# Compact chunk operands and alternating heads in the mixing stage of a flow step, with new orders in the front, the turns and the end

## The chip, the cores and the metric

The kernel runs on one core of one Trainium2 chip. The metric is the device time of one execution in microseconds (us). TensorE (PE, with its weight loads PEld) does the matmuls and the transposes, VectorE is DVE, ScalarE is ACT, GpSimd is POOL, and SyncE (SP) issues nearly all transfers.

## The reference

The reference is one inference step of a hybrid backbone for 512 latent tokens and 128 context tokens, T = 640 in all, with D = 2048. Cut to what matters:

```python
def _layer(x, mod, s0, shift_fn, lp):
    sh1, sc1, g1, sh2, sc2, g2 = jnp.split(mod, 6, axis=-1)
    h = _rmsnorm(x, lp['norm1_g']) * (1.0 + sc1) + sh1
    p = h @ lp['w_in']
    o_a, s_fin = _rwkv7_bidir(shift_fn(p[..., :C_SHIFT], lp['mu_shift']), s0, lp)
    o_b = _chunk_gmlp(jax.nn.gelu(p[..., C_SHIFT:]), lp)
    x = x + g1 * (jnp.concatenate([o_a, o_b], axis=-1) @ lp['w_out'])
    h = _rmsnorm(x, lp['norm2_g']) * (1.0 + sc2) + sh2
    ff = (jax.nn.silu(h @ lp['w_ffn_gate']) * (h @ lp['w_ffn_up'])) @ lp['w_ffn_down']
    return x + g2 * ff, s_fin
# mod = silu(c) @ w_mod + b_mod; y = _rmsnorm(x, final_norm_g)
# _rwkv7_bidir: 16 heads of 64, per direction S = S*w + (S a) b^T + v k^T, y = S r
```

## The kernel before, in words

Features lie on the 128 partitions and tokens along the free axis, in two halves of 320 (`HALF`). Most products of weights are made in three: `split` cuts a weight tile into a high and a low part, the activations have `h_hi` and `h_lo`, and `win` adds hi·hi, hi·lo and lo·hi in one PSUM tile (L188 to L190, tile `big`).

**Front.** Five token blocks are loaded and normalised (`xall`, the loop over `t`); each gets its factor `rs` from a power on GpSimd (`rsqrt`, L135), and is transposed to `xnT`. Then `quarter(g, j)` makes a quarter of the shift (g=0) or scale (g=1) of the modulation, from four `w_mod` tiles of 1 MB (L304, pool `wmp`, five buffers). `products(j)` multiplies the first blocks of `w_in`. TensorE's order is written by hand in this stage. `rows()` issues twenty small loads of parameter rows on SP at j = 1, and `params()` transposes them at j = 2.

**Mixing.** While the remaining blocks of `w_in` run as `big` products, three `Mixer` queues hand out the work on the blocks already there in small pieces between them: `take_k` makes the operands of one pair of heads and both directions, `solve` and `merge` (`pblk`, `pM`, `pT`) work on the chunks' triangular systems. A scheduler then fixes the order of the instructions on each engine. A pair of heads lies on 64 + 64 partitions; the ten chunks have 64 tokens. `R` holds two 64-wide operands of a chunk, and `XZ` (L507) the two others for each head, with zeros on the other head's partitions, so that `pG` (L636) multiplies over all 128 partitions. `pXT` (L653) are transposes of one head's rows of `XZ`, `pW` (L664) products of 64 x 64. `pmm` and `pwa` are the products for the norms and for the low-rank weights. All five take one-bank PSUM tiles of pool `pk`, which has two; a piece with both heads takes one for each. ScalarE and VectorE copy the results out (`GB`, `GR`, `GA`, `XT`, `Z`).

**FFN.** Gate, up and down are computed with seven products instead of eight for each 2 x 2 block (`seven`, products 1 to 7 in order `PORD`). The down product runs over six groups `c` of hidden blocks and eight output pairs `n`, 48 steps in all. In the last step of a group (the turn, s % 8 == 7) the operands `xd` of the next group are made: `load` brings them, `put_in` splits them, `turn_ops` says at which product. `Last` combines the seven products of the last group, `later` holds its second half (`out`, `rows`) until a product of the next step.

**End.** Sums of squares of all tokens (`sse`) are added, `rsqrt` makes `rse`, and ten outputs of 128 x 1024 follow: six on VectorE (L1976), four on ScalarE and GpSimd (L1973, L1974).

Of the kernel before, what the change touches and what calls it, by code (L numbers as in the profile page):

```python
# [57 lines left out]
FRONT = 4  # L58
REST = 6
# [28 lines left out]
def flow_step(ctx: ExitStack, tc, x_prompt, x_sample, state_rwkv, c, c_ctx, w_mod, b_mod,  # L88
# [115 lines left out]
    with ExitStack() as ph:  # L204
# [29 lines left out]
        xnT = p0.tile([P, KB, T], F32, name="xnT")  # L234
        for t in range(NT):
            xt = xall[:, t, :]
            ss = p0b.tile([P, 1], F32, name="ss")
            S.activation(junk, xt, AF.Square, accum_out=ss)
            V.tensor_scalar(ss, ss, 1.0 / D, RMS_EPS, op0=ALU.mult, op1=ALU.add)
            rs = p0b.tile([P, 1], F32, name="rs")  # L240
            rsqrt(rs, ss)
            V.tensor_scalar_mul(xt, xt, rs[:, 0:1])
            for q in range(4):
                pt = ps0.tile([P, 4, P], F32, tag="pt", name="ptx")
                for b in range(4):
                    TE.transpose(pt[:, b, :], xt[:, (4 * q + b) * P:(4 * q + b + 1) * P], ident)
                (S.copy if q % 2 else V.tensor_copy)(xnT[:, 4 * q:4 * q + 4, t * P:(t + 1) * P], pt)

# [7 lines left out]

        rowA = p0.tile([P, P], F32, name="rowA")
        rowB = p0.tile([P, P], F32, name="rowB")
        G.memset(rowB, 0.0)
        G.memset(rowA, 0.0)  # L260
        nA = C_W0

        def rows():
            for m in range(4):
                nc.sync.dma_start(rowA[C_MU + 24 * m:C_MU + 24 * m + 24, :],
                                  mu_shift[0, m, 0:3072].rearrange("(r p) -> r p", p=P))
                nc.sync.dma_start(rowA[C_MU2 + 2 * m:C_MU2 + 2 * m + 2, :],
                                  mu_shift[0, m, 3072:3328].rearrange("(r p) -> r p", p=P))
                nc.sync.dma_start(rowA[C_MU3 + m:C_MU3 + m + 1, 0:32], mu_shift[0, m:m + 1, 3328:3360])
            for off, src in ((C_W0, w0[0].rearrange("d (r p) -> (d r) p", p=P)),  # L270
                             (C_A0, a0[0].rearrange("d (r p) -> (d r) p", p=P)),
                             (C_KK, k_k[0].rearrange("(r p) -> r p", p=P)),
                             (C_KA, k_a[0].rearrange("(r p) -> r p", p=P)),
                             (C_RK, r_k[0].rearrange("(r h) n -> r (h n)", h=2)),
                             (C_GW, gn_w[0].rearrange("(r h) n -> r (h n)", h=2)),
                             (C_GB, gn_b[0].rearrange("(r h) n -> r (h n)", h=2)),
                             (C_N2, norm2_g[0].rearrange("(r p) -> r p", p=P))):
                nc.sync.dma_start(rowB[off - nA:off - nA + src.shape[0], :], src)

        def params():  # L280
            pp = ptE.tile([P, 4, P], F32, tag="ptE", name="pp")
            TE.transpose(pp[:, 0, :], rowA, ident)
            TE.transpose(pp[:, 1, :], rowB, ident)
            V.tensor_copy(prm[:, 0:nA], pp[:, 0, 0:nA])
            V.tensor_copy(prm[:, nA:C_N1], pp[:, 1, 0:C_N1 - nA])
            V.tensor_copy(prm[:, C_N2:NPRM], pp[:, 1, C_N2 - nA:NPRM - nA])

        psx.close()
        h_hi = hpool.tile([P, KB, T], F32R, tag="h_hi", name="h_hi")
        h_lo = hpool.tile([P, KB, T], F32R, tag="h_lo", name="h_lo")  # L290
        pe = pex.enter_context(tc.tile_pool(name="pe", bufs=6, space=PSUM))
        early = [[pe.tile([P, HALF], F32, tag="big", name="big") for _ in range(2)] for _ in FIRST]
# [30 lines left out]

        def products(j):
# [8 lines left out]
        for j in range(4):  # L333
            for i, _ in enumerate(itertools.chain(quarter(1, j), quarter(0, j))):
                if i in (2, 3, 4, 6, 7, 8):
                    next(prods, None)
# [10 lines left out]
            if j == 1:  # L347
                rows()
            if j == 2:
                params()  # L350
# [183 lines left out]
    def take_k(pr, p):  # L534
# [19 lines left out]
        pmm([(bones, sq)], lambda ps, s: V.tensor_scalar_max(ssq[:, s], ps, 1e-24), pk)  # L554
# [10 lines left out]
        for d in range(2):  # L565
# [5 lines left out]
            for hf in range(2):  # L571
                s = slice(HALF * hf, HALF * hf + HALF)
                two = [pk.tile([P, HALF], F32, tag="g", name="pwa") for _ in range(2)]
# [45 lines left out]
            V.tensor_mul(rev(XZ[0:64, :, 0, 1, :]), v3(tha)[0:64], i3[0:64])  # L619
# [968 lines left out]
    def seven(b11, b12, b21, b22, x, hook, nk=4, bank=fresh, last=True):  # L1588
# [10 lines left out]
        for o, i in enumerate(PORD):  # L1599
# [12 lines left out]
            if i == 3:  # L1612
                combine(b22, b22, b12)
                combine(b21, b21, b22)
# [393 lines left out]
```

## Time and profile before

| | us |
|---|---|
| median of 3 runs (3287.82 to 3290.53) | 3289.65 |
| profiled execution | 3287.43 |
| its span | 3285.6 |
| mixing stage, 165 to 1060 | 895 |

The rest of the page reads: a busy share for each engine; 40 slices of the span with the granted clock and the GB/s; then groups of instructions by line. In a group, `L636 PE MATMUL pG<-R,XZ` is line, engine, operation, output tile and operands; "x640 | 93.5, 290" is the count, busy us and mean ns of one, and behind the second bar stands the idle time of the engine ahead of them with what ended it. One matmul of full-precision operands has two records. Records of TensorE overlap, so the distance of two starts says more than a duration.

### The profile page before, as it was taken

The numbers are of one execution on the slowest core, as the hardware profiler recorded it, in microseconds if no ns is written. First come the engines' busy times: TensorE is split into PE (matmuls) and PEld (weight loads), VectorE is DVE, ScalarE is ACT, GpSimd is POOL, SyncE is SP. The second block draws the span as 40 slices with busy tenths as digits, with TensorE's granted clock in tenths as the row PEclk, the third lists the DMA queues.
The fourth block names the chain that finished last, engine by engine and source line by source line (L and its number), as shares of the span: only waits on it lengthen the run. The fifth ranks groups of instructions, "written<-read, shape, count | busy, mean of one in ns | idle before, by whom it ended". The sixth has DMA issues, their size and how long they took to land.

```text
span 3285.6 us, 72386 instructions
## 1 busy us (share of the span) xinstructions
PE 3141.3 (96%) x28216; PEld 2905.3 (88%) x28216; DVE 2401.2 (73%) x4152; ACT 1458.3 (44%) x3179; POOL 1260.1 (38%) x1098
## 2 busy tenths in 40 slices
PE   6899999999999999999999999999999999999996
PEld 3688888778887887889899999999999999999996
DVE  4447766776866677767877787777787777877787
ACT  3334444444444444346644444444444444444365
POOL 0001122221222113332166566566565555555543
PEclk9899999999999999999999999999999999999998
DMA  8767776767668588756434433433433454553453
GB/s 318 244 185 219 188 204 188 181 184 206 178 185 222 137 272 277 240 152 182 127 114 120 123 116 116 127 116 116 127 116 116 127 183 149 158 164 122 132 160 119
DMA packets 740142, 550.88 MB, mean 168 GB/s; under 512 B 140712, under 2 KB 673208, under 8 KB 730968
## 3 DMA queue, kind: packets, MB, share of 16 engines
q1 hardware_dynamic: 727480, 532.57, 54.3%
q0 software_dynamic: 9984, 13.13, 1.7%
q8 instruction: 222, 3.64, 0.5%
q14 instruction: 120, 0.98, 0.1%
q10 hardware_dynamic: 2336, 0.57, 0.1%
HBM read 437.79 MB, written 110.95 MB: 167 GB/s over the span
## 4 chain that ended last, share of the span: by engine, by line
PE 75%; DVE 9%; issue 6%; DMA 5%; POOL 3%; ACT 2%; SPq 0%; DVEq 0%; ACTq 0%; POOLq 0%
PE P L1611 15%; PE P L1609 15%; PE P L1610 15%; PE big L188 4%; PE big L190 4%; PE big L189 4%; PE pG L636 2%; PE pm L881 2%; DMA raw<-in_w_in_dram 2%; PE big L1455 1%; PE big L1456 1%; PE big L1457 1%; DMA wt<-in_w_mod_dram 1%; PE pblk L820 1%; DVE mx L781 1%
## 5 line engine op out<-in xcount | busy, mean ns | idle before, releaser
L1611 PE MATMUL P<-xo,lo 128*128 128x320 f32 x2352 | 728.1, 310 | 2.5 <-DVE lo L1397 2.5
L1609 PE MATMUL P<-xo,hi 128*128 128x320 f32 x2352 | 727.4, 309 | 0.7 <-ACT hi L1396 0.7
L1610 PE MATMUL P<-xo,hi 128*128 128x320 f32 x2352 | 727.4, 309 | 0.0
L1397 DVE TENSOR_TENSOR lo<-raw,hi 128x512 fp32r<-128x512 f32 x526 | 507.3, 967 | 171.4 <-ACT hi L1396 167.3
L1396 ACT CAST hi<-raw 128x512 fp32r<-128x512 f32 x526 | 327.2, 622 | 489.6 <-PE P L1610 388.7
L188 PE MATMUL big<-h_hi,hi 128*128 128x320 f32 x1376 | 450.8, 328 | 8.5 <-ACT hi L166 5.0
L1611 PEld LDWEIGHTS P<-xo,lo 128*128 128x128 f32 x2352 | 442.1, 188 | 3.8 <-DVE lo L1397 3.8
L1609 PEld LDWEIGHTS P<-xo,hi 128*128 128x128 f32 x2352 | 442.0, 188 | 1.0 <-ACT hi L1396 1.0
L1610 PEld LDWEIGHTS P<-xo,hi 128*128 128x128 f32 x2352 | 441.9, 188 | 0.0
L190 PE MATMUL big<-h_hi,lo 128*128 128x320 f32 x1376 | 435.1, 317 | 1.3 <-DVE lo L167 1.3
L189 PE MATMUL big<-h_lo,hi 128*128 128x320 f32 x1376 | 434.0, 315 | 0.7 <-DVE h_lo L345 0.7
L1525 POOL TENSOR_TENSOR raw<-raw 128x512 f32<-128x512 f32 x252 | 407.4, 1626 | 15.3 <-DVE lo L1397 3.9
L1611 PE MATMUL P<-xd,lo 128*128 128x320 f32 x1232 | 383.7, 311 | 13.8 <-DVE lo L1397 13.5
L1609 PE MATMUL P<-xd,hi 128*128 128x320 f32 x1232 | 381.8, 310 | 3.5 <-ACT hi L1396 1.7
L1610 PE MATMUL P<-xd,hi 128*128 128x320 f32 x1232 | 380.6, 309 | 0.0
L167 DVE TENSOR_TENSOR lo<-raw,hi 128x512 fp32r<-128x512 f32 x268 | 185.1, 693 | 204.7 <-ACT hi L166 198.3
L188 PEld LDWEIGHTS big<-h_hi,hi 128*128 128x128 f32 x1376 | 262.8, 191 | 74.0 <-issue 46.6
L166 ACT CAST hi<-raw 128x512 fp32r<-128x512 f32 x268 | 165.1, 618 | 250.8 <-PE big L189 124.8
L1396 ACT CAST hi<-rawd 128x512 fp32r<-128x512 f32 (+1 forms) x288 | 168.8, 587 | 242.1 <-PE P L1610 193.4
L190 PEld LDWEIGHTS big<-h_hi,lo 128*128 128x128 f32 x1376 | 263.2, 191 | 7.4 <-DVE lo L167 3.2
L189 PEld LDWEIGHTS big<-h_lo,hi 128*128 128x128 f32 x1376 | 263.3, 191 | 6.9 <-issue 3.5
L1611 PEld LDWEIGHTS P<-xd,lo 128*128 128x128 f32 x1232 | 231.2, 188 | 20.6 <-DVE lo L1397 20.2
(380 smaller groups left out, 6257.8 us busy)
## 6 DMA issues: line engine op xcount, KB each, us to landing
wt<-in_w_mod_dram SPq DMA_DIRECT2D x96, 1024.0 KB
raw<-in_w_ffn_gate_dram SPq DMA_DIRECT2D x182, 256.0 KB
raw<-in_w_ffn_up_dram SPq DMA_DIRECT2D x182, 256.0 KB
rec<-d_S SPq DMA_DIRECT2D x80, 576.0 KB
raw<-in_w_in_dram SPq DMA_DIRECT2D x172, 256.0 KB
rawd<-in_w_ffn_down_dram SPq DMA_DIRECT2D x128, 256.0 KB
raw<-in_w_out_dram SPq DMA_DIRECT2D x96, 256.0 KB
xd<-d_os SPq DMA_DIRECT2D x66, 320.0 KB
```

What stands on the lines that cost most here:

```text
L166: S.copy(hi, raw)
L167: V.tensor_sub(lo, raw, hi.bitcast(F32))
L188: TE.matmul(halves[hf], hi[:, k, :], h_hi[:, kb, s], start=(kb == 0), stop=False)
L189: TE.matmul(halves[hf], hi[:, k, :], h_lo[:, kb, s], start=False, stop=False)
L190: TE.matmul(halves[hf], lo[:, k, :], h_hi[:, kb, s], start=False, stop=(kb == KB - 1))
L636: TE.matmul(two[h][:, cc - c0, :], XZ[:, cc, h, :, :].rearrange("p s t -> p (s t)"), R[:, cc, :, :].rearrange("p s t -> p (s t)"), start=T ...
L1396: S.copy(hi[:, 0:nk], raw[:, 0:nk])
L1397: V.tensor_sub(lo[:, 0:nk], raw[:, 0:nk], hi[:, 0:nk].bitcast(F32))
L1525: G.tensor_tensor(out=o[:, 0:nk], in0=p[:, 0:nk], in1=q[:, 0:nk], op=ALU.subtract)
L1609: TE.matmul(ps, hi[:, k, :], xk[:, 0, :], start=f, stop=False)
L1610: TE.matmul(ps, hi[:, k, :], xk[:, 1, :], start=False, stop=False)
L1611: TE.matmul(ps, lo[:, k, :], xk[:, 0, :], start=False, stop=l)
```

## The change

There are four parts.

In the front, `quarter(1, 0)` is made ahead of the token loop as a generator (`lead`), and from block `t` = `BEGIN` on the loop takes one step of it; `rows()` is issued on GpSimd, behind the loop in the code; `params()` comes at j = 1.

In the mixing, `XZ` becomes `X` without zeros. `pG` multiplies each head's 64 partitions on their own, h = 0 and h = 1 in turn. Pool `pk` has one two-bank tile (`both`), taken by `pmm`, `pwa`, `pG`, `pXT` and `pW`.

In the turns, `put_in(1)` is done one step earlier (s % 8 == 6), into pool `xd2` in every second group, and `load(c + 1, ...)` earlier to match.

At the end, the last step has its own class `End` and order `PEND`: it finishes tokens 3 and 4 before its last two products, then tokens 0 to 2; the ten outputs go 3, 4, 0, 1, 2, nine on VectorE alone.

```diff
+BEGIN = 2
+PEND = (1, 6, 7, 5, 4, 3, 2)
...
-                nc.sync.dma_start(rowA[C_MU + 24 * m:C_MU + 24 * m + 24, :],
+                nc.gpsimd.dma_start(rowA[C_MU + 24 * m:C_MU + 24 * m + 24, :],
...
+        lead = quarter(1, 0)
         for t in range(NT):
...
+            if t >= BEGIN:
+                next(lead)
+        rows()
...
-            for i, _ in enumerate(itertools.chain(quarter(1, j), quarter(0, j))):
+            for i, _ in enumerate(itertools.chain(lead if j == 0 else quarter(1, j), quarter(0, j))):
...
             if j == 1:
-                rows()
-            if j == 2:
                 params()
...
+    def both(name):
+        return pk.tile([P, 2, 512], F32, tag="g", name=name)
+
-    def pmm(rhs_list, evac, pool, tag="g"):
+    def pmm(rhs_list, evac):
+        two = both("pmm")
         for hf in range(2):
-            ps = pool.tile([P, HALF], F32, tag=tag, name="pmm")
+            ps = two[:, hf, 0:HALF]
...
-    XZ = bz.tile([P, NCH, 2, 2, CH], F32, name="XZ")
-    for h in range(2):
-        G.memset(XZ[hsl(h), :, 1 - h], 0.0)
+    X = bz.tile([P, NCH, 2, CH], F32, name="X")
...
-            V.tensor_mul(rev(XZ[0:64, :, 0, 1, :]), v3(tha)[0:64], i3[0:64])
+            V.tensor_mul(rev(X[0:64, :, 1, :]), v3(tha)[0:64], i3[0:64])
...
-                two = [pk.tile([P, 4, P], F32, tag="g", name="pG") for _ in range(2)]
+                two = both("pG").rearrange("p h (c t) -> p h c t", t=P)
+                two = [two[:, h] for h in range(2)]
                 for cc in range(c0, c1):
                     for h in range(2):
-                        TE.matmul(two[h][:, cc - c0, :], XZ[:, cc, h, :, :].rearrange("p s t -> p (s t)"),
-                                  R[:, cc, :, :].rearrange("p s t -> p (s t)"), start=True, stop=True)
+                        TE.matmul(two[h][:, cc - c0, :], X[hsl(h), cc].rearrange("p s t -> p (s t)"),
+                                  R[hsl(h), cc].rearrange("p s t -> p (s t)"), start=True, stop=True)
...
-                        TE.transpose(two[h][:, cc - c0, :], XZ[s, cc, h, :, :].rearrange("p s t -> p (s t)"), ident[s, s])
+                        TE.transpose(two[h][:, cc - c0, :], X[s, cc].rearrange("p s t -> p (s t)"), ident[s, s])
...
-    pk = pbx.enter_context(tc.tile_pool(name="pk", bufs=2, space=PSUM))
+    pk = pbx.enter_context(tc.tile_pool(name="pk", bufs=1, space=PSUM))
...
-        return {1: ((put_in, 1), (load, c, 6)), 3: ((put_in, 2), (direct, c, 3)), 5: ((put_in, 7), (direct, c, 5))}
+        return {1: ((load, c, 6),), 3: ((put_in, 2), (direct, c, 3)), 5: ((put_in, 7), (direct, c, 5))}
...
-            if s % 8 == 6 and c < NC - 1 and o in (2, 3, 4):
-                load(c + 1, (1, 2, 7)[o - 2])
+            if s % 8 == 5 and c < NC - 1 and o == 2:
+                load(c + 1, 1)
+            if s % 8 == 6 and c < NC - 1 and o in (3, 4):
+                load(c + 1, (2, 7)[o - 3])
+            if s % 8 == 6 and c < NC - 1 and o == 1:
+                put_in(1, later_x, c % 2 == 0)
...
+    class End(Last):
...
+            elif o == 4:
+                self.put(0, 1, p, cs)
+                pr = pP.tile([P, 2, 256], F32, tag="P", name="prd")
+                self.turn(pr, 0, 3, (1, 0))
+                self.turn(pr, 1, 4, (1, 0))
+                S.copy(acc[:, n, 768:1280].rearrange("p (t c) -> p t c", c=256), pr)
+                for t in range(2):
+                    self.square(pr[:, t], sse[:, 3 + t, n:n + 1])
+                scale(3, 5, 8)
+            elif o > 4:
...
+                for t in range(3):
+                    self.turn(pr[t // 2], t % 2, t, (m,))
...
+                if not m:
+                    scale(0, 3, 9)
...
-    for t in range(NT):
-        for h in range(2):
+    for t in (3, 4, 0, 1, 2):
+        for h in (1, 0):
...
-            if t == 1 or t == 3:
-                S.activation(out, src, AF.Copy, scale=rs[:, t:t + 1])
-                G.tensor_tensor(out=out, in0=out, in1=f, op=ALU.mult)
+            if h and t in EARLY:
+                S.activation(out, src, AF.Copy, scale=rse[:, t:t + 1])
```

How the scheduler's order moves shows best in three places. On TensorE in the mixing, with the `pXT` transposes between `big` products (L188 to L190), before:

```order
L636 MATMUL pG<-R,XZ 128x128 [waits DVE_49,PE_49]
L636 MATMUL pG<-R,XZ 128x128
L190 MATMUL big<-h_hi,lo 128x320
L653 MATMUL pXT<-ident,XZ 128x64 [waits DVE_49,PE_49]
L653 MATMUL pXT<-ident,XZ 128x64 x7
L188 MATMUL big<-h_hi,hi 128x320
L189 MATMUL big<-h_lo,hi 128x320
L190 MATMUL big<-h_hi,lo 128x320
L188 MATMUL big<-h_hi,hi 128x320
L189 MATMUL big<-h_lo,hi 128x320
L653 MATMUL pXT<-ident,XZ 128x64 [waits Activation_49]
L653 MATMUL pXT<-ident,XZ 128x64 x7
```

and after, where the lines of `big` are L189 to L191:

```order
L191 MATMUL big<-h_hi,lo 128x320 [waits DVE_49]
L662 MATMUL pXT<-ident,X 128x64 [waits DVE_49,PE_49,Activation_49]
L662 MATMUL pXT<-ident,X 128x64 x15
L189 MATMUL big<-h_hi,hi 128x320
L190 MATMUL big<-h_lo,hi 128x320
L191 MATMUL big<-h_hi,lo 128x320
```

Eight transposes of one head and, later, eight of the other have become one piece of sixteen that alternates between the heads. Over the program the 320 `pXT` stood in 49 such pieces and stand in 32; the 320 `pG` matmuls stood in 80 and stand in 58; `pW` has 32 both times.

In the front, before, SP issues the parameter rows (`rowA`, `rowB`) between the weights `wt` and `raw`:

```order
L304 DMA wt<-in_w_mod_dram 128x4x512
L265 DMA rowA<-in_mu_shift_dram 24x128
L267 DMA rowA<-in_mu_shift_dram 2x128
L269 DMA rowA<-in_mu_shift_dram 1x32
...
L278 DMA rowB<-in_gn_b_dram 8x128
L278 DMA rowB<-in_norm_g_dram 16x128
L304 DMA wt<-in_w_mod_dram 128x4x512 x3
```

and after, GpSimd's queue has them, between the powers `rs` of the token loop:

```order
L136 TENSOR_TENSOR rs<-ss,mhalf 128x1
L294 DMA rowB<-in_w_dram 16x128
L281 DMA rowA<-in_mu_shift_dram 24x128
L283 DMA rowA<-in_mu_shift_dram 2x128
L285 DMA rowA<-in_mu_shift_dram 1x16x2
L281 DMA rowA<-in_mu_shift_dram 24x128
L283 DMA rowA<-in_mu_shift_dram 2x128
L285 DMA rowA<-in_mu_shift_dram 1x16x2
L136 TENSOR_TENSOR rs<-ss,mhalf 128x1
```

The loads stand behind the loop in the code, but the scheduler puts them between the powers; the third and fourth power have six issues ahead of them each. SP's `wt` loads follow each other.

On VectorE at the end, before, one reduction for all tokens stands ahead of the outputs:

```order
L1886 TENSOR_TENSOR cd<-P_40115,tp 128x320 [waits PE_49]
L1859 SCALAR_TENSOR_TENSOR cd<-cd,modc_90,x1d 128x192 [waits DVE_49]
L1859 SCALAR_TENSOR_TENSOR cd<-cd,modc_90,x1d 128x128
L1964 TENSOR_REDUCE rse<-sse 128x5 [waits Activation_49]
L1965 TENSOR_SCALAR rse<-rse 128x5 [waits DVE_49]
L1976 SCALAR_TENSOR_TENSOR out<-acc,rse 128x1024 [waits DMAHW3_49,DMAHW4_49,DMAHW0_49,Pool_49]
L1976 SCALAR_TENSOR_TENSOR out<-acc,rse 128x1024 x5
```

and after:

```order
L1936 SCALAR_TENSOR_TENSOR cd<-P_39967,modc_90,cd 128x320 [waits DVE_49,PE_49]
L2001 TENSOR_REDUCE rse<-sse 128x2 [waits Activation_49]
L2002 TENSOR_SCALAR rse<-rse 128x2 [waits DVE_49]
L2077 SCALAR_TENSOR_TENSOR out<-acc,rse 128x1024 [waits DMAHW4_49,DMAHW5_49,DMAHW0_49,Pool_49]
L1936 SCALAR_TENSOR_TENSOR cd<-P_40001,modc_90,cd 128x320 [waits PE_49]
L2077 SCALAR_TENSOR_TENSOR out<-acc,rse 128x1024 x2
L2001 TENSOR_REDUCE rse<-sse 128x3 [waits Activation_49]
L2002 TENSOR_SCALAR rse<-rse 128x3 [waits DVE_49]
L2077 SCALAR_TENSOR_TENSOR out<-acc,rse 128x1024 [waits Pool_49]
```

Three outputs of tokens 3 and 4 now come ahead of the reduction for the other three tokens, one of them ahead of the last product's `cd`.

More of the change, by code (lines that the diff above doesn't have):

```diff
@@ L254, in flow_step @@
         V.tensor_copy(prm[:, C_N1:C_N2], pp[:, 0, 32:48])
[L257 to L292, printed above, removed]
         mc = p0.tile([P, 2, KB, 2], F32, name="mc")
@@ L324, in products @@
+        h_lo = hpool.tile([P, KB, T], F32R, tag="h_lo", name="h_lo")
+        pe = pex.enter_context(tc.tile_pool(name="pe", bufs=6, space=PSUM))
+        early = [[pe.tile([P, HALF], F32, tag="big", name="big") for _ in range(2)] for _ in FIRST]
         def products(j):
@@ L572, in take_k @@
                 s = slice(HALF * hf, HALF * hf + HALF)
-                two = [pk.tile([P, HALF], F32, tag="g", name="pwa") for _ in range(2)]
+                pwa = both("pwa")
+                two = [pwa[:, h, 0:HALF] for h in range(2)]
                 for h in range(2):
@@ L648, in take_k @@
             for (c0, c1) in ((0, 8), (8, NCH)):
-                two = [pk.tile([P, 8, CH], F32, tag="g", name="pXT") for _ in range(2)]
+                two = both("pXT").rearrange("p h (c t) -> p h c t", t=CH)
+                two = [two[:, h] for h in range(2)]
                 for cc in range(c0, c1):
```

180 lines of the change are left out of this document (136 added, 44 removed).

## The prediction

> **What bounds the kernel now.** First the page, for which engine is the bound.
>
> ```profile
> span 3285.6 us, 72386 instructions
> PE 3141.3 (96%) x28216; PEld 2905.3 (88%) x28216; DVE 2401.2 (73%) x4152; ACT 1458.3 (44%) x3179; POOL 1260.1 (38%) x1098
> ```
>
> TensorE is the bound as a whole: 3285.6 - 3141.3 = 144 us are left idle, and every matmul that gets shorter or goes away may count. The change touches four stages, and each has a limit of its own, so next the windows view, by stage. Its columns are the stretch and its length in us, the busy time of PE, PEld, DVE, ACT and POOL, the granted clock, the DMA share and GB/s.
>
> ```profile
> 30.00:40.00 10.00, 7.32 (x64) 1.68 (x62) 1.94 (x8) 1.22 (x3) 0.00 (x0) 1.00 0.75 264
> 40.00:50.00 10.00, 6.62 (x36) 1.03 (x28) 3.72 (x9) 1.97 (x3) 0.00 (x0) 0.66 1.05 383
> 60.00:70.00 10.00, 9.46 (x68) 5.35 (x67) 1.22 (x4) 1.20 (x2) 0.00 (x0) 1.00 0.64 221
> 70.00:80.00 10.00, 3.62 (x21) 1.62 (x20) 6.91 (x15) 2.88 (x4) 0.00 (x0) 0.82 0.69 237
> 165.00:1060.00 895.00, 858.77 (x9478) 728.56 (x9477) 622.44 (x1187) 391.88 (x850) 185.28 (x281) 0.98 0.71 193
> 3270.00:3280.00 10.00, 0.00 (x0) 0.00 (x0) 10.00 (x5) 0.00 (x0) 8.94 (x3) 0.50 0.77 307
> ```
>
> The front is limited by transfers: at full share they bring 383 GB/s, and there are three dips, to 264, 221 and 237. The mixing stage (165 to 1060) is TensorE's, with 895.0 - 858.8 = 36 us idle. The end has no TensorE work at all, only VectorE, GpSimd and the transfers of the output.
>
> **Part A, the front.** In the queue's timeline (start and length in us, then the line and what moves) the twenty loads of parameter rows begin here, and the next weight load stands behind all twenty:
>
> ```profile
> 57.10 1.16 SPq L265 DMA_DIRECT2D rowA<-in_mu_shift_dram  x1
> 72.32 1.49 SPq L304 DMA_DIRECT2D wt<-in_w_mod_dram  x3
> ```
>
> SP is held for 72.32 - 57.10 = 15.2 us, and that is when the transfers dip. Missing in the two stretches: (383 - 221) + (383 - 237) = 308 GB/s over 10 us, 3.1 MB, or 8 us at 383 GB/s. The dip at 30 to 40 comes ahead of the first quarter of the modulation: the weight buffers (five) are full until the products of the first quarter empty them, and these now begin inside the token loop. It lacks (383 - 264) x 10 us = 1.2 MB, 3 us. Together 11; I take **-9**, since the small loads still have to move. The twenty issues go to GpSimd, where the powers of the token loop run, some of them now behind six or seven issues. The rows for that:
>
> ```profile
> 14.18 0.57 POOL L135 TENSOR_TENSOR rs<-ss,mhalf 128x1 f32<-128x1 f32 x1 [3.20 <-DVE ss L239]
> 267.35 4.32 POOL L672 DMA_DIRECT2D dd<-GB  x8 [11.90 <-ACT GB L641]
> ```
>
> An issue costs 4.32 / 8 = 0.54 us there, six or seven of them 3.2 to 3.8, and GpSimd stood idle for 3.2 before such a power. So they are about covered, and weights land later than the tokens anyway. If that cover is gone, half of 20 x 0.54 = 10.8 us is on the path. Bounds: -11 and +6.
>
> **Part B, the mixing.** `X` drops the zeros, so a product inside a chunk uses one head's 64 partitions instead of all 128, and the two heads can run side by side. What the pieces cost comes from the timeline of TensorE, by the distance of starts; a piece stands between products of the projection (`big`). First the alternating kind, which the kernel has already in `pW`:
>
> ```profile
> 243.50 0.31 PE L190 MATMUL big<-h_hi,lo 128*128 128x320 f32 x1
> 243.79 0.31 PE L189 MATMUL big<-h_lo,hi 128*128 128x320 f32 x1
> 244.03 0.80 PE L664 MATMUL pW<-Z,GA 64*64 64x64 f32 x20
> 244.76 0.42 PE L190 MATMUL big<-h_hi,lo 128*128 128x320 f32 x1
> 245.01 0.31 PE L188 MATMUL big<-h_hi,hi 128*128 128x320 f32 x1
> ...
> 266.01 0.31 PE L188 MATMUL big<-h_hi,hi 128*128 128x320 f32 x1
> 266.15 0.61 PE L636 MATMUL pG<-R,XZ 128*128 128x128 f32 x4
> 266.51 0.39 PE L189 MATMUL big<-h_lo,hi 128*128 128x320 f32 x1
> 266.75 0.31 PE L190 MATMUL big<-h_hi,lo 128*128 128x320 f32 x1
> ```
>
> Two `big` starts lie (243.79 - 243.50) / 2 = 0.145 apart. Over 243.79 to 245.01 lie two of them and the piece: 1.22 - 0.29 = 0.93 us for 20 records of `pW`. Over 266.01 to 266.75: 0.74 - 0.29 = 0.45 for four records of `pG`, 0.1125 each. This piece has full rows like its neighbours. Then the transposes:
>
> ```profile
> 445.94 0.30 PE L188 MATMUL big<-h_hi,hi 128*128 128x320 f32 x1
> 446.17 0.71 PE L653 MATMUL pXT<-ident,XZ 64*128 64x64 f32 x8
> 446.81 0.42 PE L189 MATMUL big<-h_lo,hi 128*128 128x320 f32 x1
> 447.06 0.31 PE L190 MATMUL big<-h_hi,lo 128*128 128x320 f32 x1
> ...
> 448.78 0.31 PE L190 MATMUL big<-h_hi,lo 128*128 128x320 f32 x1
> 449.02 0.34 PE L653 MATMUL pXT<-ident,XZ 64*128 64x64 f32 x2
> 449.28 0.41 PE L188 MATMUL big<-h_hi,hi 128*128 128x320 f32 x1
> 449.54 0.31 PE L189 MATMUL big<-h_lo,hi 128*128 128x320 f32 x1
> ```
>
> Eight of one head: 1.12 - 0.29 = 0.83; two: 0.76 - 0.29 = 0.47. So 0.06 for each transpose of one head, and 0.35 for going to half rows and back. With it `pW` gives (0.93 - 0.35) / 20 = 0.029 for an alternating record, half of 0.06: two heads side by side.
>
> ```profile
> L636 PE MATMUL pG<-R,XZ 128*128 128x128 f32 x640 | 93.5, 290 | 18.3 <-DVE XZ L619 14.2 <-DVE GA L644 2.3 <-DVE XZ L622 1.5
> L653 PE MATMUL pXT<-ident,XZ 64*128 64x64 f32 x320 | 29.8, 238 | 1.3 <-DVE GA L644 1.0 <-ACT XT L657 0.2
> ```
>
> `pG` before: 640 x 0.1125 = 72.0 and no change of rows. After, its matmuls stand in 58 pieces: 58 x 0.35 = 20.3, plus a first record in each that nothing overlaps, 58 x 0.11 = 6.4, plus 320 x 0.1125 = 36.0 for pairs side by side; 62.7, or -9. `pXT` before: 49 pieces, 49 x 0.35 + 320 x 0.06 = 36, less about 2 where a piece holds both heads, 34. After, 32 pieces that alternate: 32 x 0.35 + 320 x 0.03 = 21, or -13. `pW` keeps its 32 pieces. TensorE's own work shrinks by 22 to 23 us. The trace of before has no half-row `pG`, so the price is between that of two heads fully side by side and that of none (rivals). How much is realised: `pG` waited 14.2 us for the writes of `XZ` on VectorE, whose writes keep their length; a TensorE that is ahead by 23 us meets these later. I take two thirds, -15. One two-bank tile also means that the second half of `pmm` and of `pW` and each new tile wait for both evacuations; behind that wait stand the `big` products in TensorE's order. I put +2 on it. **-13**, bounds -25 and +19.
>
> [...]
>
> **Part C, the turns of the last product stage.** Loading `xd` costs VectorE this, in the middle of a turn:
>
> ```profile
> 2920.57 4.60 DVE L1671 TENSOR_TENSOR xd<-opd,xd 128x320 fp32r<-128x320 f32 x3
> ...
> PE P L1611 <- DVE lo L1397: 9.4, 12, 1.7
> ```
>
> The second row is from the waits of TensorE between 2700 and 3200: 9.4 us for the low halves of weights that VectorE splits. One of the operands is made a step earlier, which moves work of that size out of the turn. VectorE has no more idle time there than here, so I take under half: **-4**, bounds -9 and +2.
>
> **Part D, the end.** Rows of VectorE and GpSimd at the end, then the chain that ended last:
>
> ```profile
> 3259.53 0.49 DVE L1886 TENSOR_TENSOR cd<-P,tp 128x320 f32<-128x320 f32 x1
> 3265.51 15.70 DVE L1976 SCALAR_TENSOR_TENSOR out<-acc,rse 128x1024 f32<-128x1024 f32 x6 [1.29 <-POOL rse L135]
> 3266.74 12.20 POOL L1974 TENSOR_TENSOR out<-out,acc 128x1024 f32<-128x1024 f32 x4 [1.26 <-ACT out L1973]
> ...
> 3265.51 1.29 DVE out L1976
> ```
>
> From the last product to the end: 3285.6 - 3259.5 = 26.1 us, of it 6.0 to the scale. Alone an output operation takes 1.29, beside GpSimd's 15.70 / 6 = 2.6. Now GpSimd takes none, and three of the ten outputs are made before the last product's tokens are turned. What is late next is the transfer: the output is 640 x 2048 x 4 bytes = 5.24 MB, 17 us at the 307 GB/s of the window above; seven tenths of it 12 us. So 6.0 + 1.3 + 12 = 19, or -7; the sums in the last step may hold TensorE for 1 us more. **-6**, bounds -12 and 0.
>
> **Sum.** -9 - 13 - 4 - 6 = -32. The profiled execution took 3287.4 us, so 3255.4; the median of the runs lies 2.2 above it: **3258 us**. A measurement of this kernel can tell about 0.2%, 6.6 us, from no change: faster ends at 3283.1, slower starts at 3296.2.
>
> **The rivals.**
>
> VectorE keeps its pace in the mixing (0.11): the 14.2 us of waits for `XZ` grow by what TensorE saves, B is 0, and the time is 3271. For it speaks that wait; against it, VectorE is busy for only 622 of 895 us.
>
> The front waits for GpSimd's queue (0.05): A is +6, the time 3273. For it: 3.2 to 3.8 us of issues against 3.2 idle; against it: weights are what the front waits for.
>
> Loads in line within a head (0.05): each `pG` matmul takes 0.1125 + 0.06 = 0.1725, 320 of them 55.2, with the changes of rows 75.5 (+3.5); `pXT` at 0.06 gives 30 (-4); with the +2 B is +2, the time 3273. [...]
>
> The heads don't overlap at all in `pG` (0.06): 20.3 + 72.0 = 92.3, +20; `pXT` -4, waits +2; B is +19, the time 3290, no change. Against it stands the 0.029 of `pW`; for it, that `pG` is twice as wide as anything seen in half rows.
>
> Slower: the single two-bank tile puts TensorE behind the evacuations (0.10). There are 8 tiles in a direction and 2 more in a pair, 16 x 8 + 8 x 2 = 144 turnovers, and one evacuation takes
>
> ```profile
> 263.84 0.37 ACT L641 COPY GB<-pG 64x256 f32<-64x256 f32 x1 [2.42 <-PE pG L636]
> ```
>
> 0.37 us: 144 x 0.37 = +53, so 3311. It decides from 32 / 144 = 0.22 us a turnover on, and is slower beyond noise from 0.27. For it: TensorE's order is fixed, so a wait there holds the products behind it. Against it: before, too, each piece of two heads took both tiles, and the order places products between.
>
> My own forecast keeps 0.63. The range 3236 to 3280 leaves out the last two rivals (0.16) and the edges of the forecast's case; its low end is the sum with B at its full -25 and the rest near their bounds. Faster: 0.63 + 0.11 + 0.05 + 0.05 = 0.84; within 0.2%: 0.06; slower: 0.10.
>
> **What would show it.** Right: transfers near 383 GB/s throughout 30 to 80 us; `pG` at 0.056 a record; waits of TensorE for `X` below 25 us; VectorE's waits in the turns at about 5 us; 19 us from the last product to the end. Wrong: waits of TensorE for ACT or VectorE at `pG`, `pXT` and `pW` adding up to tens of us (the slower rival), `pG` records starting 0.11 apart (no overlap), or the token loop ending later than before.

## The result, and the profile after

The changed kernel takes 3278.78 us (median of five runs, 3271.51 to 3281.16) against 3289.65 before: a ratio of 0.9959, with a 95% interval of 0.9945 to 0.9972. A second series gave 0.9972 (0.9961 to 0.9983). It is faster by about 9 to 13 us; 32 were forecast. The profiled execution took 3273.31. Its page begins:

```profile
span 3271.5 us, 72372 instructions
PE 3109.1 (95%) x28216; PEld 2863.4 (88%) x28216; DVE 2394.8 (73%) x4160; ACT 1454.8 (44%) x3181; POOL 1259.4 (38%) x1113
```

TensorE is busy for 32 us less, yet the span fell by only 14. The windows of the changed kernel, first those of the front:

```profile
30.00:40.00 10.00, 7.32 (x64) 2.24 (x61) 2.46 (x7) 1.76 (x3) 0.00 (x0) 1.00 1.05 384
60.00:70.00 10.00, 9.52 (x68) 5.40 (x67) 3.52 (x10) 2.35 (x4) 0.00 (x0) 1.00 1.04 385
70.00:80.00 10.00, 6.90 (x39) 4.16 (x36) 5.75 (x14) 3.46 (x6) 0.00 (x0) 0.83 1.07 369
```

The three dips of the transfers are gone (384, 385 and 369 GB/s instead of 264, 221 and 237). For the mixing stage a window between two fixed times would not do: in it less busy time is more idle time by definition. So here is the stretch between the same two products of the projection (the 300th and the 4000th of `big`), before and after:

```profile
152.00:1113.80 961.80, 922.94 (x10155) 787.16 (x10154) 666.08 (x1263) 415.05 (x891) 196.29 (x299) 0.98 0.70 191
```

```profile
140.20:1111.10 970.90, 896.93 (x10155) 746.29 (x10154) 674.95 (x1265) 417.25 (x894) 191.94 (x299) 0.98 0.69 190
```

Over this stretch TensorE is busy for 26 us less, and idle for 970.9 - 896.9 = 74.0 us instead of 961.8 - 922.9 = 38.9, 35 more. The stage takes 9 us longer, and of the 11.8 us by which it starts earlier, 2.7 are left at its end. How far ahead the changed kernel is shows in the times of the same products, here the modulation's `pm` that run beside the projection (the two times at the end of the part before the semicolon are the first and the last start), before and after:

```profile
L881 PE MATMUL pm<-wt,cT x512: 591/592/761, 149.1 to 1087.1; 128*2 128x512 f32 x171
```

```profile
L891 PE MATMUL pm<-wt,cT x512: 591/592/1061, 137.3 to 1080.3; 128*2 128x512 f32 x171
```

The front has won 149.1 - 137.3 = 11.8 us; at the last of these products 6.8 are left. The end of the changed kernel, from its timeline:

```profile
3254.43 1.28 DVE L2077 SCALAR_TENSOR_TENSOR out<-acc,rse 128x1024 f32<-128x1024 f32 x1 [0.82 <-POOL rse L136]
3254.65 0.31 PE L1628 MATMUL P<-xd,lo 128*128 128x320 f32 x1
3256.09 2.47 DVE L2077 SCALAR_TENSOR_TENSOR out<-acc,rse 128x1024 f32<-128x1024 f32 x2
3259.83 7.26 DVE L2077 SCALAR_TENSOR_TENSOR out<-acc,rse 128x1024 f32<-128x1024 f32 x6 [0.97 <-POOL rse L136]
```

From the start of the last product to the end it is 3271.5 - 3254.65 = 16.9 us. Before, that product starts at 3259.2:

```profile
L1611 PE MATMUL P<-xd,lo x1232: 302/309/418, 2674.6 to 3259.2; 128*128 128x320 f32 x176
```

so it was 26.4, and the end has won 9.5. An output operation takes 7.26 / 6 = 1.21 us where it took 2.6 beside GpSimd.

Where the added waits in the mixing stage are, the groups of TensorE between 153 and 1110 us tell. Before (the rows of `pG` and `pXT` are those of the prediction, with 18.3 and 1.3 us):

```profile
L664 PE MATMUL pW<-Z,GA 64*64 64x64 f32 x640 | 25.5, 223 | 0.2 <-ACT XT L657 0.2
L501 PE MATMUL pmm<-fs,bones 128*128 128x320 f32 x32 | 12.5, 474 | 0.0
L501 PE MATMUL pmm<-sqk,bones 128*128 128x320 f32 x32 | 10.2, 443 | 0.4 <-ACT sqk L551 0.4
```

After:

```profile
L644 PE MATMUL pG<-R,X 64*128 64x128 f32 x640 | 59.8, 306 | 25.8 <-DVE GA L652 10.7 <-DVE X L626 8.9 <-ACT hi L167 3.2
L674 PE MATMUL pW<-Z,GA 64*64 64x64 f32 x640 | 26.3, 226 | 5.1 <-issue 2.7 <-ACT XT L666 2.4
L662 PE MATMUL pXT<-ident,X 64*128 64x64 f32 x320 | 17.4, 237 | 6.5 <-DVE GA L652 4.2 <-ACT XT L666 1.5 <-ACT A__1115 L816 0.6
L509 PE MATMUL pmm<-fs,bones 128*128 128x320 f32 x32 | 13.1, 493 | 11.6 <-DVE zv L689 10.3 <-ACT Z L676 1.3
L509 PE MATMUL pmm<-sqk,bones 128*128 128x320 f32 x32 | 12.2, 464 | 2.9 <-ACT sqk L557 2.9
```

The idle time ahead of these operations, which share the two-bank tile, was 18.3 + 1.3 + 0.2 + 0.4 = 20.2 us and is 25.8 + 5.1 + 6.5 + 11.6 + 2.9 = 51.9. Most of the waits after are for copies out of the tile (`GA`, `zv`, `XT`, `Z`: 30 us). One such place in the timeline of TensorE:

```profile
438.18 1.16 PE L644 MATMUL pG<-R,X 64*128 64x128 f32 x16 [2.66 <-DVE GA L652]
441.99 1.22 PE L644 MATMUL pG<-R,X 64*128 64x128 f32 x8 [2.65 <-ACT hi L167]
443.14 0.63 PE L189 MATMUL big<-h_hi,hi 128*128 128x320 f32 x1
443.58 0.47 PE L190 MATMUL big<-h_lo,hi 128*128 128x320 f32 x1
443.84 0.47 PE L191 MATMUL big<-h_hi,lo 128*128 128x320 f32 x1
```

Pieces of `pG` follow each other with no `big` between, and TensorE stands idle for 2.66 and 2.65 us at the turnover. Of the waits for `X`, 8.9 us are in the row of `pG`, and the list of waits has two more rows:

```profile
PE pG L644 <- DVE X L630: 1.4, 2, 0.9
PE pG L644 <- DVE X L629: 1.3, 1, 1.3
```

That is 11.6 us, where it was 14.2 + 1.5 = 15.7.

### The profile page after: what moved, and what is told of

It is laid out like the page before. It is cut to its first block, busy times and chain, and to the rows that moved or that the text cites. A ratio compares the mean times of both kernels' runs of the same rounds, so it can differ in the third digit from the quotient of the medians.

```text
span 3271.5 us, 72372 instructions
## 1 busy us (share of the span) xinstructions
PE 3109.1 (95%) x28216; PEld 2863.4 (88%) x28216; DVE 2394.8 (73%) x4160; ACT 1454.8 (44%) x3181; POOL 1259.4 (38%) x1113
## 4 chain that ended last, share of the span: by engine, by line
PE 72%; DVE 11%; DMA 6%; issue 6%; POOL 3%; ACT 3%; SPq 0%; DVEq 0%; POOLq 0%; ACTq 0%
PE P L1628 15%; PE P L1626 15%; PE P L1627 15%; PE big L189 4%; PE big L191 4%; PE big L190 4%; PE pm L891 2%; DMA wt<-in_w_mod_dram 1%; DVE lo L1408 1%; PE big L1466 1%; PE big L1467 1%; PE big L1468 1%; PE pG L644 1%; PE big L1023 1%; DVE lo L168 1%
## 5 line engine op out<-in xcount | busy, mean ns | idle before, releaser
L1408 DVE TENSOR_TENSOR lo<-raw,hi 128x512 fp32r<-128x512 f32 x526 | 497.7, 949 | 176.2 <-ACT hi L1407 171.7
L189 PE MATMUL big<-h_hi,hi 128*128 128x320 f32 x1376 | 451.6, 328 | 9.4 <-ACT hi L167 6.0
L191 PE MATMUL big<-h_hi,lo 128*128 128x320 f32 x1376 | 435.5, 318 | 2.3 <-DVE lo L168 2.0
L190 PE MATMUL big<-h_lo,hi 128*128 128x320 f32 x1376 | 434.6, 316 | 0.5 <-DVE h_lo L351 0.5
L189 PEld LDWEIGHTS big<-h_hi,hi 128*128 128x128 f32 x1376 | 263.5, 191 | 83.5 <-issue 56.5
L168 DVE TENSOR_TENSOR lo<-raw,hi 128x512 fp32r<-128x512 f32 x268 | 184.0, 690 | 164.6 <-ACT hi L167 156.1
L191 PEld LDWEIGHTS big<-h_hi,lo 128*128 128x128 f32 x1376 | 262.6, 191 | 11.0 <-DVE lo L168 5.6
L190 PEld LDWEIGHTS big<-h_lo,hi 128*128 128x128 f32 x1376 | 263.8, 192 | 6.2 <-DVE h_lo L351 1.1
```

What stands on the lines that cost most here:

```text
L168: V.tensor_sub(lo, raw, hi.bitcast(F32))
L189: TE.matmul(halves[hf], hi[:, k, :], h_hi[:, kb, s], start=(kb == 0), stop=False)
L190: TE.matmul(halves[hf], hi[:, k, :], h_lo[:, kb, s], start=False, stop=False)
L191: TE.matmul(halves[hf], lo[:, k, :], h_hi[:, kb, s], start=False, stop=(kb == KB - 1))
L1408: V.tensor_sub(lo[:, 0:nk], raw[:, 0:nk], hi[:, 0:nk].bitcast(F32))
```

## The experiments

Each time is a median; the ratio is to the runs of the kernel before in the same series, with its interval. Waits are those of TensorE between 153 and 1110 us of one profile (between the same two products their sums come out within 5 us of that). The length of the mixing stage is counted between the 300th and the 4000th product of the projection in every profile. Theory 1 is, where an expectation doesn't say otherwise, that the single tile's turnover eats part B; theory 2 is that TensorE no longer sets the pace of the stage. The changed kernel itself ran in two of the series (0.9959 and 0.9972); where an experiment ran in another, the comparison with it goes by the ratios.

**The old mixing in the new kernel.** `X` is padded again, `pk` has two one-bank tiles; front, turns and end stay changed.

```diff
-    X = bz.tile([P, NCH, 2, CH], F32, name="X")
+    XZ = bz.tile([P, NCH, 2, 2, CH], F32, name="XZ")
-                two = both("pG").rearrange("p h (c t) -> p h c t", t=P)
-                two = [two[:, h] for h in range(2)]
+                two = [pk.tile([P, 4, P], F32, tag="g", name="pG") for _ in range(2)]
```

> The changed kernel with the mixing part undone (padded XZ, full-row pG, two one-bank tiles in pk); front, turns and end stay changed. Theory 1 (the single two-bank tile makes TensorE wait in the mixing stage, and that eats the whole of part B and more): the offset of -11.8 us that stood at 165 us in the changed kernel's profile is kept through the mixing, and with -2 to -4 of the stages behind it and -9.6 of the end the median is 3264 to 3268, below the changed kernel. Rival (part B paid, and the time was lost elsewhere): part B's gain is missing, 3285 to 3292.

3278.0 us, 0.9952 (0.9939 to 0.9966): as fast as the changed kernel. Neither expectation held. Part B is worth nothing, between +2 and +7 us by the ratios (0.9959 and 0.9972 against 0.9952), and what is left over is less than front and end show in the profile. The waits are near those of before, 48 us in all, and 17.9 + 1.6 + 0.2 + 0.8 = 20.5 ahead of `pG`, `pXT`, `pW` and `pmm`. The first two of these rows:

```profile
L640 PE MATMUL pG<-R,XZ 128*128 128x128 f32 x640 | 92.4, 288 | 17.9 <-DVE XZ L623 14.4 <-DVE GA L648 1.8 <-DVE XZ L626 1.5
L657 PE MATMUL pXT<-ident,XZ 64*128 64x64 f32 x320 | 29.6, 238 | 1.6 <-DVE GA L648 0.8 <-ACT XT L661 0.5
```

**Compact `X` in two one-bank tiles.** Only the second hunk above.

> The changed kernel with compact X, but pk again as two one-bank tiles, one for each head; the order then has one head's products in a row. Theory 1: the waits for evacuations fall back to those of before (about 34 us of TensorE's waits in the mixing instead of 70), but without alternation pG pays for 80 changes of rows and no overlap, up to 80 x 0.35 + 640 x 0.11 = 100 us against 72: between 3264 (heads overlap anyhow) and 3294. Rival (compact X alone brings the loss, whatever the tile): as slow as the changed kernel or slower, with waits of about 70.

3305.96 us, 1.0039 (1.0026 to 1.0052). That is 29 us more than with the old mixing. TensorE's order is that of before, one head after the other, and the waits are too; `pG` is dearer:

```profile
L638 PE MATMUL pG<-R,X 64*128 64x128 f32 x640 | 98.2, 316 | 18.6 <-DVE X L621 14.3 <-DVE GA L646 2.5 <-DVE X L624 1.5
```

By the 0.35 us that the prediction worked out for going to half rows and back, 80 pieces would be 28 us, an estimate that is about the difference. The granted clock was lower too, 0.977 to 0.981 over the six runs against 0.986 to 0.988 with the old mixing, so how much of the 29 us is the change of rows is not shown. The time is 12 us above the 3294 expected, about as far as the kernel with the old mixing is above its own expectation. The waits sum to 43 us: compact `X` alone does not bring them.

**Padded `XZ` in the two-bank tile.** Only the first hunk. TensorE's pieces stand in the order of the changed kernel, so the difference to it is that of half rows in `pG` alone, and the difference to the old mixing is the tile with its order.

> The changed kernel with padded XZ and full-row pG again, in the single two-bank tile and in the same order of pieces. Theory 1: the waits for the tile stay (60 us or more in the mixing) and pG's 9 us of gain go, 3282 to 3290. Rival (half-row products are the cost): faster than the changed kernel, 3265 to 3273.

3291.59 us, 0.9999 (0.9990 to 1.0009). Against the changed kernel half rows bring 0.27 to 0.40%, 9 to 13 us, where the prediction had 9 for `pG`. Against the old mixing (0.9952, same series) the two-bank tile, with the order that the scheduler makes for it, costs 0.47%, 15 us, although its transposes are cheaper. Theory 1 holds but for 2 us (3282 to 3290 were expected): the users of the tile wait here as in the changed kernel, with full rows and `X` padded:

```profile
L646 PE MATMUL pG<-R,XZ 128*128 128x128 f32 x640 | 90.4, 291 | 23.9 <-DVE XZ L628 8.9 <-ACT hi L167 6.2 <-DVE GA L654 5.6
L676 PE MATMUL pW<-Z,GA 64*64 64x64 f32 x640 | 26.1, 226 | 2.2 <-ACT XT L668 2.1
L664 PE MATMUL pXT<-ident,XZ 64*128 64x64 f32 x320 | 17.5, 237 | 9.1 <-DVE GA L654 4.9 <-ACT XT L668 2.2 <-ACT A__1117 L818 1.9
L509 PE MATMUL pmm<-fs,bones 128*128 128x320 f32 x32 | 13.2, 496 | 9.6 <-DVE zv L691 9.0 <-ACT Z L678 0.5
L509 PE MATMUL pmm<-sqk,bones 128*128 128x320 f32 x32 | 12.6, 476 | 2.9 <-ACT sqk L559 2.9
```

Together 23.9 + 2.2 + 9.1 + 9.6 + 2.9 = 47.7 us, 27 more than the 20.5 of the old mixing. Other waits of the stage are shorter, so that all of them sum to 63 us against 48, 15 more, like the time.

**Both halves ahead of the copies.** `pmm` and `pW` fill both halves of the tile before either is copied.

```diff
-            evac(ps, s)
+        for hf in range(2):
+            evac(two[:, hf, 0:HALF], slice(HALF * hf, HALF * hf + HALF))
```

> The changed kernel, but pmm and pW issue the products of both halves of the two-bank tile ahead of the evacuations of either. Theory 1: the waits of pmm (14.5 us) and of pW (5.1 us) for the other half's evacuation go, two thirds of it realised: 3264 to 3269. Rival (TensorE is only early there and waits for the same thing a moment later): within 3 us of the changed kernel.

3275.52 us, 0.9944 (0.9932 to 0.9957): the lowest ratio of all, though its interval overlaps that of the changed kernel's first series, and it is 3 us below its median, not the 10 to 15 that theory 1 had. The waits at `pmm` went from 14.5 to 10.1 only, those at `pW` from 5.1 to 2.6; now the first products of the next turn wait for the copies of the one before:

```profile
L509 PE MATMUL pmm<-fs,bones 128*128 128x320 f32 x32 | 11.8, 495 | 1.0 <-ACT Z L678 0.9
L509 PE MATMUL pmm<-sqk,bones 128*128 128x320 f32 x32 | 11.7, 492 | 9.1 <-DVE zv L691 7.5 <-ACT sqk L558 1.6
```

**The front alone.** The kernel before with the front part of the diff.

> The kernel before with the front part of the change alone. Theory 1 (the 11.5 us of the front are a plain shift of all that follows): 3277 to 3280. Rival (the mixing stage gives part of it back even in its old form, as the profile of the kernel with the old mixing suggests, where 12 us went between 165 and 1120 us): 3281 to 3287.

3284.52 us, 0.9981 (0.9969 to 0.9994), 2 to 10 us. In its profile 12 us are kept through the mixing, and 10.5 to the last product; its runs spread from 3277 to 3290, and the profiled one is the lowest of them.

**Without the turns' part.** `put_in(1)` back in the turn.

> The changed kernel with the turns of the down product as before (the operands of product 1 are split in the turn again). Between the product records 6750 and 10807 the four profiles with the changed turns lost 1.0 to 7.7 us against before. Theory 1 (the turns' part is a loss of 3 us): 1 to 4 us below the changed kernel, with that stretch within 1.5 us of before. Rival (the turns' part gains, and the loss there comes from the last step): up to 4 us above it.

3282.38 us, 0.9976 (0.9965 to 0.9988). The intervals overlap those of the changed kernel, so whether the turns' part gains or loses is not decided.

**Two two-bank tiles.**

```diff
-    pb = pbx.enter_context(tc.tile_pool(name="pb", bufs=3, space=PSUM))
-    pk = pbx.enter_context(tc.tile_pool(name="pk", bufs=1, space=PSUM))
-    pt_ = pbx.enter_context(tc.tile_pool(name="pt_", bufs=2, space=PSUM))
+    pb = pbx.enter_context(tc.tile_pool(name="pb", bufs=2, space=PSUM))
+    pk = pbx.enter_context(tc.tile_pool(name="pk", bufs=2, space=PSUM))
+    pt_ = pbx.enter_context(tc.tile_pool(name="pt_", bufs=1, space=PSUM))
```

> The changed kernel with two two-bank tiles in pk; the banks come from the projection's pool pb (2 instead of 3) and from the transposes' pool pt_ (1 instead of 2). Theory 1 (the single tile's turnover is what eats part B): TensorE's waits at pG, pmm, pXT and pW in the mixing fall from about 50 us to 25, and the time from 3279 to about 3262, unless big and the transposes now wait: then their rows show it. Rival (TensorE only meets the writes of X and the evacuations' engines earlier): the waits move to DVE X and stay at 70 in all, within 4 us of the changed kernel.

3279.82 us, 0.9965 (0.9948 to 0.9982): no gain. The groups show the first half of the expectation right, and where the waits went:

```profile
L191 PE MATMUL big<-h_hi,lo 128*128 128x320 f32 x1208 | 383.0, 319 | 13.0 <-DVE lo L168 12.7
L644 PE MATMUL pG<-R,X 64*128 64x128 f32 x640 | 58.7, 295 | 11.1 <-DVE GA L652 5.3 <-DVE X L626 4.7 <-ACT gq L702 0.8
L509 PE MATMUL pmm<-fs,bones 128*128 128x320 f32 x32 | 12.4, 469 | 0.2 <-ACT Z L676 0.2
```

`pmm` waits 0.2 us and `pG` 11.1, so the tile's waits are more than halved; the products of the projection, which have one bank less, now wait 13.0 for the low halves of their weights, from 1.5. All waits of TensorE in the stage sum to 70.4 us against 73.1.

**The rows on SP again,** the lead kept.

> The changed kernel with the twenty row loads on SP at their old place, and the params step with them; the first quarter stays in the token loop. By the prediction's working of the front: 3 of the 11.5 us stay, 8 go, so that the projection's products start 3 to 4 us ahead of before at 150 us instead of 11.5, with the transfers at 220 to 240 GB/s again between 55 and 80 us.

One execution, 3293.92 us, above the median of before (3289.62 in its series) in spite of the lead; a single time says little here. The `pm` products start 5 to 6 us ahead of before, and this window has the gap again:

```profile
60.00:70.00 10.00, 8.69 (x61) 5.97 (x56) 2.38 (x7) 1.22 (x3) 0.00 (x0) 1.00 0.29 76
```

So about 6 us of the front belong to the row loads and 5 to the lead, where 8 and 3 were worked out. At 30 to 40 us this kernel, too, has 385 GB/s.

**More buffers behind the copies:** `GR` six, `XT` three; and the same with both halves first.

```diff
-GR = bk.tile([P, 4, CH], F32, tag="GR", name="GR", bufs=2)
+GR = bk.tile([P, 4, CH], F32, tag="GR", name="GR", bufs=6)
```

> The changed kernel with six buffers for GR (two before) and three for XT (two), so that the copies out of the two-bank tile wait less for the stores of earlier copies (20 us of VectorE's and 23 us of ScalarE's waits in the mixing). Theory 2 (the mixing stage goes at the pace of the chain of copies, stores and VectorE, not of TensorE): TensorE's waits fall from 73 us towards 60 and the time to 3268 to 3274. Rival (the tile itself, or TensorE's work, sets the pace): within 4 us of the changed kernel.

> Both repairs together: pmm and pW issue both halves ahead of their evacuations, and GR has six buffers, XT three. If the two act on different waits the gains add up: 3262 to 3270. If the waits only move on, as with two tiles: 3273 to 3280.

3296.92 us, 1.0023 (1.0011 to 1.0034), and 3294.47, 1.0011 (1.0000 to 1.0023): both slower than the changed kernel, and the first slower than before, which no theory said. The scheduler laid another order, and the waits of the stage rose from 73 to 84 us in the first and 80 in the second, in the first at `pW` above all:

```profile
L674 PE MATMUL pW<-Z,GA 64*64 64x64 f32 x640 | 28.7, 240 | 12.1 <-ACT XT L666 8.0 <-ACT Z L676 4.1
```

**28 us of TensorE work added,** after and before.

```diff
+                    for _ in range(3):
+                        TE.matmul(two[h], wr[:, h, d, :], wa[:, h, s], start=False, stop=False)
```

> The changed kernel with 28 us of TensorE work added in the mixing: the low-rank residual product is issued four times instead of once (192 more products of 0.147 us; the residual is counted fourfold in the result). Theory 2 (TensorE no longer sets the pace there, since its waits took up what it saved): well under 28 us more, 5 to 18. Rival (TensorE sets it): 24 to 32 more.

> The kernel before with the same 28 us of TensorE work added (residual counted fourfold). With TensorE busy for 859 of 895 us both theories expect nearly all of it: 20 to 30 us more. If it is far less here too, the mixing stage had slack on TensorE already before the change, and part B could never have brought its 22 us.

3315.82 us, 1.0084 (1.0060 to 1.0108), 37 to 41 us above the changed kernel by the ratios; and 3317.01, 1.0076 (1.0060 to 1.0092), 25 above before. Theory 2, which had 5 to 18, falls in this form: behind the change, too, added work is paid in full. Waits did fall, to 61 us, but not the time. One reservation stands: the added products are those of `pwa`, which hold the two-bank tile, so they lengthen its turn as well, and the run can't tell the pace of TensorE from the pace of the tile.

**`pmm` out of the two-bank tile,** into one-bank tiles of `pt_`, with no bank taken from another pool.

> The changed kernel with pmm in one-bank tiles of the transposes' pool pt_, so that it neither takes nor waits for the two-bank tile; no bank is taken from another pool. If the waits at the single tile are a cost of their own, pmm's 14.5 us of waits fall below 5 and the time by 6 to 12 us, to 3267 to 3273. If waits only move on to the next product in TensorE's order, as with two tiles, the sum stays above 65 and the time within 4 us of the changed kernel.

3292.01 us, 1.0003 (0.9989 to 1.0018). `pmm` waits 5.7 us instead of 14.5, as the first theory had it, but the sum is 76.2, and the time is 9 us above the 3282.76 of the changed kernel in the same series. Its profile is of a slower execution (3297.82) and has more busy time of TensorE between the same products, 911 us instead of 897, at a granted clock of 0.95 there instead of 0.98:

```profile
L673 PE MATMUL pW<-Z,GA 64*64 64x64 f32 x640 | 27.6, 234 | 9.2 <-ACT XT L665 8.7 <-ACT Z L675 0.3
L508 PE MATMUL pmm<-sqk,bones 128*128 128x320 f32 x32 | 11.6, 475 | 4.5 <-DVE mx L790 3.8 <-ACT sqk L556 0.7
```

**Second profiles of both kernels and of the front alone.**

> The kernel before, unchanged, for a second profile beside one chip's other runs. If the front alone is worth only 5 us in the median because the first profile of before was slow in the front, its products of the projection start 5 to 6 us earlier than in the first profile at 150 us; if the mixing stage scatters from one execution to the next, the front repeats within 1 us, and the time from 165 to 1120 us differs by up to 12.

> The changed kernel, unchanged, for a second profile: the front repeats at -11 to -12 us and the end at -9.6; the mixing stage may differ by some us, and the waits at pG, pXT, pW and pmm stay near 50 us if they belong to the order and not to one execution.

> The kernel with the front part alone, for a second profile. In its first profile the mixing stage took as long as before (962 us between the same products) and the 12 us of the front held to the end; the same mixing code took 974 us in the kernel with the old mixing. If the stage scatters after the earlier start, this profile lies between 962 and 974; if that belongs to the other parts, at 962.

Before repeats (3290.33, 0.9996, 0.9985 to 1.0007): front and mixing within 1 us. The changed kernel's front repeats (-12). Its mixing took 8 us longer this time, with the same waits at the tile: 5.5 of the 8 are busy time of TensorE (902.45 us instead of 896.93 between the same products), at a granted clock of 0.97 instead of 0.98. The front alone keeps 9 us to the last product in its second profile (3278.71 us). The old mixing code took 962 us behind the new front three times in four, and 974 once, with 6 us more of waits and 4 to 5 more of busy time; why, and why the median of the front alone is only 6 us below before, stays open.

**Front and end only.** Mixing and turns of before.

> The changed kernel with the mixing and the turns of before: only the front and the end are changed. If parts B and C bring nothing, it is as fast as the changed kernel or faster: 3272 to 3278. If the turns' part gains, it is above the kernel with the old mixing (3278) by up to 4.

3274.08 us, 0.9959 (0.9946 to 0.9972): the whole gain of the change, without its mixing and its turns.

## Why the prediction was wrong

The step that failed is in part B: "I put +2 on it", for what one two-bank tile adds in waits. The profile has 51.9 us of idle time ahead of the tile's users against 20.2, so 32 instead of 2. With the operands held the same (padded `XZ`, two-bank tile against one-bank tiles) it is 47.7 against 20.5, so 27 of the 32 belong to the tile with its order; that tile made the kernel 15 us slower, its cheaper transposes included. The half rows of `pG` bring 9 to 13 back, and so B is worth nothing, where -13 was forecast.

The slower rival named this mechanism with its break-even of 0.22 us for each of 144 turnovers; 31.7 / 144 is 0.22. It got 0.10. What I put against it, that before too each piece took both tiles, did not look at how they come free: one bank at a time, so the next piece's first head could begin while the second was still being copied. The order of before reads like that, with the split by head that I counted as a cost; no run tests this reading by itself.

That the kernel gained 11 us even so is owed to the front and the end. For part B it is luck, then, that 3278.78 lies inside the range of 3236 to 3280; the median of the second series, 3282.76, lies outside.

The tile's turnover is not the whole cause, though. Two edits took away more than half of the waits that they aimed at (two tiles, `pmm` elsewhere) and one a third of them (both halves first), and the sum of waits stayed at 68 to 76 us. With one-bank tiles it was 38 to 48 in every kernel, with two-bank tiles 61 to 84. That the two-bank tile, with its order, adds some 27 us of waits at its users is shown; how much is its turnover and how much the order that the scheduler lays for it, and through which of its choices the waits move on, is not.

Point by point: **The front** was forecast at -9 and has -11.8 in the profile; the cover held, though not wholly: the last transposes of the tokens start 0.9 us later (30.9 instead of 30.0 us; 28.7 in the run with the rows on SP). The token loop ending later was named as a sign of being wrong; it came true, and the front gained all the same. Its 8 and 3 were 6 and 5. How much of it reaches the end in the median is less sure (6, interval 2 to 10). **Half rows** were rightly forecast as side by side. Sixteen alternating transposes:

```profile
447.87 0.31 PE L189 MATMUL big<-h_hi,hi 128*128 128x320 f32 x1
448.11 0.71 PE L662 MATMUL pXT<-ident,X 64*128 64x64 f32 x16
448.75 0.42 PE L190 MATMUL big<-h_lo,hi 128*128 128x320 f32 x1
449.01 0.31 PE L191 MATMUL big<-h_hi,lo 128*128 128x320 f32 x1
```

449.01 - 447.87 - 0.29 = 0.85 us, against 0.35 + 16 x 0.03 = 0.83 worked out. And eight records of `pG`:

```profile
665.43 0.71 PE L644 MATMUL pG<-R,X 64*128 64x128 f32 x8
666.07 0.42 PE L189 MATMUL big<-h_hi,hi 128*128 128x320 f32 x1
```

The next product starts 666.07 - 665.43 = 0.64 us behind the first of them, where eight at 0.1125 one after the other would be 0.90. `pG` and `pXT` together have 77 us of busy time instead of 123, and by the pair of kernels in one order half rows are worth 9 to 13 us, as forecast. So of the rivals, the heads that don't overlap and the loads in line fall. No run shows the 0.06 us that the latter added to each `pG` matmul for its loads: half rows were to make `pG` 3.5 us dearer by it, and took 9 to 13 us off the time. The cut by a third for late writes of `X` was needless: those waits fell from 15.7 us to 11.6. VectorE's pace was the wrong rival for the right result of B. **The turns** were forecast at -4; TensorE's waits for low halves between 2640 and 3260 are the same, before and after:

```profile
PE P L1611 <- DVE lo L1397: 13.9, 19, 1.7
```

```profile
PE P L1628 <- DVE lo L1408: 15.0, 20, 1.7
```

so the move freed no wait there; in the medians the turns are worth 0 to -6. **The end** was forecast at -6 with 19 us behind the last product; it has 16.9, -9.5, of which the last step's own stalls take 1 to 3 back.

With 0 for B and C the prediction's own sum would have been -15, and the time about 3275; front and end alone measured 3274.08.

## What to carry to other kernels

Here two one-bank tiles, freed one by one, were 15 us better than one tile of two banks with the order laid for it, though a piece of two heads takes two banks in either case: before joining such tiles, count the turnovers and price each by the copies that now stand ahead of it, since here some two tenths of a us, 144 times, outweighed what alternation saved. And where a scheduler lays the order, an idle time that a profile names is not yet a gain to be had: three repairs here took away the named wait or part of it, and nearly as much stood elsewhere in the new order. Test the repair, and judge it by the time, with the sum of waits beside it. Count that sum between the same two products before and after, since in a window of fixed times busy and idle time only mirror each other.

## What the runs showed of the hardware

Behind two waits of TensorE here the products ran slower for a time. After the waits at 438 and 442 us the products of the projection start 0.267 us apart (443.84 - 443.58 is 0.26 in the rows above), until

```profile
446.51 0.35 PE L189 MATMUL big<-h_hi,hi 128*128 128x320 f32 x1
446.69 0.31 PE L190 MATMUL big<-h_lo,hi 128*128 128x320 f32 x1
446.84 0.31 PE L191 MATMUL big<-h_hi,lo 128*128 128x320 f32 x1
```

and from there 0.148 apart again (446.69 to 447.87 us, eight distances). The granted clock between 440 and 450 us is 0.67:

```profile
440.00:450.00 10.00, 8.01 (x54) 7.49 (x54) 4.53 (x11) 4.09 (x10) 4.28 (x8) 0.67 0.99 274
```

Within it, the clock is 0.50 from 443 to 446.5 us and 0.99 from 446.5 to 450. Eleven distances of 0.267 instead of 0.148 are 1.3 us, on top of the 5.3 waited. The waits were 2.66 and 2.65 us, with 1.16 us of `pG` between. The full pace came back 4.5 us after the second wait ended at 441.99, and 446.51 - 443.14 = 3.4 us after the first product of the projection behind it. This is one place in one profile: that the waits brought the lower clock is read from the order of the two, and from what length of wait on it comes, or after how much work it goes, is not shown.
